# The SSD stage of a fused two-layer kernel: pacing of the group chains against the next group's GEMM

## The chip, the cores and the metric

One core of a Trainium2 chip runs the whole program. The metric is the device time of one launch in microseconds. Three runs of the kernel before gave 1353.03, 1350.03 and 1352.99 us, median 1352.99 us.

## The reference, cut to what matters

Two blocks run one after the other on 512 tokens of width 1024. The second block has an attention branch, a state-space (SSD) branch and a mixture of experts. The change touches only the SSD branch, which is (with the parts that do not matter here left out):

```python
xbc = silu(causal_depthwise_conv(xbc, conv_w, conv_b))       # 4 taps
xs, bs, cs = split(xbc, [2048, 2560])
dt = softplus(dt_raw + dt_bias); A = -exp(a_log)
y = ssd_chunked(xs.reshape(B, T, 32, 64), dt, A, bs, cs)     # 4 groups of 8 heads, state 128
y = y + d_skip * xs
yf = y * silu(z)                                             # per group of 512 columns:
y = yf * rsqrt(mean(yf * yf) + eps) * ssd_norm
merged = sigmoid(gate_a) * (y_attn @ w_attn_branch) + sigmoid(gate_b) * (y @ w_ssd_branch)
```

All values are float32. Every large matrix product is made of three products of rounded halves (high times high, high times low, low times high), so each weight tile is first split into a high and a low part.

## The kernel before, in words

The SSD branch is worked off in four groups g = 0 to 3 of 512 columns. For each group there are three kinds of work.

`ssd_gemm(g)` (line 1191) is the input projection: five units of `gemm_t` (line 210), each two output columns of 128 wide. Unit 0 gives B and C, units 1 and 2 give x, units 3 and 4 give z. A unit is 48 matmuls of 128x512 on TensorE (lines 224 to 226) and yields after every 12 of them with the planned time 12 x 0.217 = 2.604 us. Such a stretch of 12 matmuls is called a piece here, so a unit is 4 pieces and `ssd_gemm` 20. When a unit is complete its `done` function runs: for units 0 to 2 `conv_silu` (line 1169), which on VectorE is L1177, three L1183 and L1189 per output column, and for units 3 and 4 `silu_from` (L450 and L455 on VectorE per column).

`ssd_chain(g)` (line 1222) is the recurrence. Four time chunks c of 128 tokens pass through three stages in a software pipeline of six steps (`pipeline`, line 458). Stage s0 fetches the decay rows (DMA from `scr_a`, tile `ab`, two buffers) and transposes x and B on TensorE (L1245, L1249, L1247). Stage s1 subtracts per head on VectorE (eight L1265), takes the exponential on ScalarE (L1267) and multiplies (L1270). Stage s2 has the products L1278, L1283 and L1295 on TensorE, which VectorE evicts (L1280, L1290, L1297), and GpSimd adds (L1298). Then comes the gated norm: GpSimd multiplies y by z four times (L1303), ScalarE squares (L392), VectorE adds the squares (L393), TensorE sums them over partitions (L369, `rms_col`), VectorE and GpSimd make the reciprocal root (L372, L374), TensorE broadcasts it (L382), and VectorE scales and splits the four tiles (four L1311, four L356, beside ScalarE's L355) into `yh` and `yl`.

`ssd_branch(g)` (line 1320) is the output projection of a group from `yh` and `yl`: four GEMMs of 24 matmuls, 8 pieces in all.

The order in which this is written out comes from `mix(main, filler)` (line 32): the chain yields a need in planned microseconds, and pieces of the filler are written until the need is paid; a surplus is carried over. In `block2b` (line 1339) the filler of chain g is `ssd_branch(g - 1)` followed by `ssd_gemm(g + 1)`; `block2m` (line 1349) does the last chain, with `ssd_branch(2)`, two attention projections of 8 pieces each (`attn`) and the loads for them as filler. Each engine works through its own queue in order. The program is built with a planner (`schedule_with_timeline_sim`) that replays the written order and, on each engine, takes the earliest written instruction that it holds to be ready; so the order of a queue follows the written order, except that an instruction that the planner holds to be late is passed by later ones. The order is fixed when the program is built.

Of the kernel before, what the change touches and what calls it, by code (L numbers as in the profile page):

```python
# [24 lines left out]
KK = ([0, 1, 2, 3], [4, 5, 6, 7])  # L25

def run(gen):
    for _ in gen:
        pass


def mix(main, filler):

    debt = 0
    for need in main:
        debt += need
        while debt > 0:
            t = next(filler, None)
            if t is None:
                break  # L40
            debt -= t


class Ker:
# [1146 lines left out]
    def ssd_gemm(self, g, hh, hl, rb, rbh):  # L1191

        nc = self.nc
        u2 = lambda i: [("w2", 2 * (8 + 5 * g + i)), ("w2", 2 * (8 + 5 * g + i) + 1)]
        d = self.grp[g] = {}

        def bc_done(ps):
            d["b"], d["c"] = self.t2(), self.t2()
            self.conv_silu(ps, (16 + g, 20 + g), (d["b"], d["c"]), rb)

        def xs_done(i):
            def f(ps):
                if i == 0:
                    d["xs"], d["y"] = self.t8(), self.t8()
                self.conv_silu(ps, (4 * g + 2 * i, 4 * g + 2 * i + 1), (d["xs"][:, 2 * i], d["xs"][:, 2 * i + 1]), rb)
                for j in (2 * i, 2 * i + 1):
                    nc.scalar.activation(d["y"][:, j], d["xs"][:, j], AF.Copy, scale=self.pv("d_skip", 4 * g + j))
            return f

        d["z"] = self.mm[g % 2 * 4:g % 2 * 4 + 4]  # L1210

        def z_done(i):
            def f(ps):
                self.silu_from(ps, rbh, d["z"][2 * i:2 * i + 2])
            return f
        yield from self.gemm_t(u2(0), hh, hl, KK, bc_done)
        for i in range(2):
            yield from self.gemm_t(u2(1 + i), hh, hl, KK, xs_done(i))
        for i in range(2):
            yield from self.gemm_t(u2(3 + i), hh, hl, KK, z_done(i))  # L1220

    def ssd_chain(self, g, need):
        nc = self.nc
        d = self.grp[g]
        xs, y, bT, cT = d["xs"], d["y"], d["b"], d["c"]
# [76 lines left out]
        for k in range(4):  # L1302
            nc.gpsimd.tensor_tensor(y[k], d["y"][:, k], y[k], op=ALU.mult)  # L1303
            self.acc_sq(ssq, y[k], k == 0)
        yield need
        r = self.rms_col(ssq, NT, 512)
        yield 2.6
        pr = self.bcast_rows(r, NT)
        d["yh"], d["yl"] = [], []
        for k in range(4):  # L1310
# [27 lines left out]

    def block2b(self, hh, hl, rb, rbh):
        self.grp = {}  # L1340
        f = self.ssd_gemm(0, hh, hl, rb, rbh)
        mix(self.ssd_prep(), f)
        run(f)
        for g in range(3):
            f = chain(*([self.ssd_branch(g - 1)] if g else []), self.ssd_gemm(g + 1, hh, hl, rb, rbh))
            mix(self.ssd_chain(g, 4.0), f)
            run(f)

    def block2m(self):

        nc = self.nc
        yah, yal = [], []
        ma = self.mm

        def load():
            yt = [self.t8(F32R) for _ in range(2)]
            for k in range(8):
                t_ = self.t2()
                nc.sync.dma_start(t_, self.yad[k])
                h, l = self.split(t_, hi=yt[k // 4][:, k % 4])  # L1360
                yah.append(h)
                yal.append(l)
                yield 0

        def attn(g):
            for t_, i in zip(ma[2 * g:2 * g + 2], range(2)):
                nc.sync.dma_start(t_, self.gd[2 * g + i])

            def f(ps):
                for t_, p in zip(ma[2 * g:2 * g + 2], ps):  # L1370
                    nc.vector.scalar_tensor_tensor(t_, t_, 1.0, p, op0=ALU.add, op1=ALU.mult)
            yield from self.gemm_t([("wab", 2 * g), ("wab", 2 * g + 1)], yah, yal, KK, f)

        f = chain(self.ssd_branch(2), load(), attn(0), attn(1))
        mix(self.ssd_chain(3, 4.0), f)
        run(f)
        run(attn(2))
        run(attn(3))
        gb = []

        def fetch():
            t_ = self.t2()
            nc.sync.dma_start(t_, self.gd[8 + len(gb)])
            gb.append(t_)
        for _ in range(4):
            fetch()
        mh, ml, mt = [], [], []

        def merge(k):
            t_ = gb[k]  # L1390
            m = self.mB[k]
            nc.vector.scalar_tensor_tensor(m, t_, 1.0, m, op0=ALU.add, op1=ALU.mult)
            nc.vector.tensor_tensor(m, m, ma[k], op=ALU.add)
            if k % 4 == 0:
                mt.append(self.t8(F32R))
            h, l = self.split(m, hi=mt[k // 4][:, k % 4])
            mh.append(h)
            ml.append(l)
            if k < 4:
                fetch()  # L1400
        run(self.ssd_branch(3, lambda c: (merge(2 * c), merge(2 * c + 1))))
        return mh, ml
# [799 lines left out]
```

## Time and profile before

The span is cut into engines; a row of windows gives, for a stretch of the span, its length, the busy time of each engine with the number of instructions, the granted clock of TensorE as a share of full speed, the DMA share and the rate.

| | |
|---|---|
| median of 3 runs | 1352.99 us |
| the profiled execution | 1348.09 us |
| its span | 1346.1 us |
| TensorE busy | 1263.8 us, 94% |
| VectorE busy | 869.1 us, 65% |
| ScalarE busy | 506.3 us, 38% |
| GpSimd busy | 436.5 us, 32% |
| DMA, mean | 167 GB/s |

The SSD stage lies between about 555 us (first GEMM of group 0) and about 1020 us of the span; the chains of groups 0 to 3 begin at 611.3, 692.0, 792.7 and 893.1 us. After it come the output projection, the router and the experts, which read their weights at over 400 GB/s up to the end.

### The profile page before, as it was taken

What the parts mean: (1) busy time and instruction counts of PE and PEld (TensorE: products, weight loads), DVE (VectorE), ACT (ScalarE), POOL (GpSimd) and SP (SyncE); (2) the same over time, 40 slices, a digit from 0 to 9 for tenths busy, and PEclk for the clock granted to TensorE, in tenths of its full rate; (3) what the DMA queues carried; (4) which work ended last, traced back from release to release, by engine and by line L of the source; (5) the groups of instructions that cost most, each with busy time, mean ns of one, the idle gap of its engine ahead of it and who ended that gap; (6) DMA issues with size and microseconds to landing.
All of it is one profiled execution on the core that took longest, in us unless ns stands there. A gap on an engine that the chain in (4) does not pass through costs nothing.

```text
span 1346.1 us, 18784 instructions
## 1 busy us (share of the span) xinstructions
PE 1263.8 (94%) x6992; PEld 976.4 (73%) x6992; DVE 869.1 (65%) x1648; ACT 506.3 (38%) x938; POOL 436.5 (32%) x467
## 2 busy tenths in 40 slices
PE   5959999999999999999989899999999999999897
PEld 5858888999987888888767787787889744334223
DVE  5596765767998667687977887877683522111116
ACT  4545453345544455354442442443333211111011
POOL 5473134159343431122444234234415200000011
PEclk8979999999999999999989899899999899999999
DMA  7324232142233221134325235376420699999994
GB/s 249 110 65 141 63 120 97 51 156 80 65 117 110 79 95 63 56 112 133 90 83 133 78 102 126 110 246 174 140 106 37 234 403 417 401 415 415 415 414 182
DMA packets 87342, 224.86 MB, mean 167 GB/s; under 512 B 7840, under 2 KB 31040, under 8 KB 87248
## 3 DMA queue, kind: packets, MB, share of 16 engines
q1 hardware_dynamic: 79808, 203.08, 44.0%
q10 hardware_dynamic: 4992, 11.83, 2.3%
q0 software_dynamic: 2448, 8.72, 1.8%
q8 instruction: 56, 0.92, 0.3%
q14 instruction: 38, 0.31, 0.1%
HBM read 205.97 MB, written 17.63 MB: 166 GB/s over the span
## 4 chain that ended last, share of the span: by engine, by line
PE 63%; DVE 20%; DMA 10%; issue 4%; ACT 2%; POOL 1%; SPq 0%; ACTq 0%; DVEq 0%; POOLq 0%
PE pmm L224 9%; PE pmm L226 9%; PE pmm L225 9%; PE pmm L1740 7%; PE pmm L1761 5%; DMA t<-scr_a 4%; DVE t L1265 2%; PE paux L1078 2%; DVE t L1010 2%; DMA wr<-in_we_dram 2%; DMA tb<-in_we_dram 2%; DVE m L1009 1%; PE paux L1727 1%; DVE wlo L175 1%; PE pmm L242 1%
## 5 line engine op out<-in xcount | busy, mean ns | idle before, releaser
L175 POOL TENSOR_TENSOR wlo<-tb,whi 128x1024 fp32r<-128x1024 f32 x78 | 199.0, 2552 | 329.0 <-ACT whi L173 300.7
L224 PE MATMUL pmm<-tb,whi 128*128 128x512 f32 x600 | 240.0, 400 | 1.8 <-DVE t L903 1.8
L226 PE MATMUL pmm<-tb,wlo 128*128 128x512 f32 x600 | 239.1, 399 | 0.0
L225 PE MATMUL pmm<-tb,whi 128*128 128x512 f32 x600 | 238.8, 398 | 0.0
L173 ACT CAST whi<-tb 128x1024 fp32r<-128x1024 f32 x139 | 145.0, 1047 | 148.9 <-PE pmm L225 69.6
L224 PEld LDWEIGHTS pmm<-tb,whi 128*128 128x128 f32 x600 | 115.0, 192 | 25.4 <-DVE t L903 2.2
L226 PEld LDWEIGHTS pmm<-tb,wlo 128*128 128x128 f32 x600 | 115.1, 192 | 24.3 <-issue 0.5
L225 PEld LDWEIGHTS pmm<-tb,whi 128*128 128x128 f32 x600 | 114.9, 192 | 23.3 <-issue 0.4
L175 DVE TENSOR_TENSOR wlo<-tb,whi 128x1024 fp32r<-128x1024 f32 x61 | 81.8, 1343 | 26.0 <-ACT whi L173 25.8
L224 PE MATMUL pmm<-t,whi 128*128 128x512 f32 (+1 forms) x208 | 79.2, 393 | 12.4 <-DVE t L610 12.4
L225 PE MATMUL pmm<-t,whi 128*128 128x512 f32 (+1 forms) x208 | 80.3, 390 | 0.9 <-DVE t L356 0.8
L226 PE MATMUL pmm<-t,wlo 128*128 128x512 f32 (+1 forms) x208 | 80.2, 389 | 0.0
L1747 DVE SCALAR_TENSOR_TENSOR th<-th,pmm 128x256 f32<-128x256 f32 x16 | 6.7, 420 | 106.6 <-ACT th L1746 106.6
L1265 DVE TENSOR_SCALAR t<-t,acs 128x128 f32<-128x128 f32 x128 | 54.7, 493 | 19.6 <-DMA t<-scr_a 19.6
L1183 DVE SCALAR_TENSOR_TENSOR t<-cv,cwh,t 128x512 f32<-128x512 f32 x72 | 61.3, 901 | 0.3 <-ACT t L1180 0.3
L1740 PE MATMUL pmm<-wr,xe 128*64 128x512 f32 x200 | 57.8, 598 | 1.5 <-DMA wr<-in_we_dram 1.5
L1679 POOL COPY wcol<-wrow 32x2 f32<-32x2 f32 x64 | 11.9, 186 | 137.3 <-DVE y L1773 58.7
L334 PE MATMUL pmm<-whi,tb 128*128 128x256 f32 x192 | 54.7, 285 | 0.0
L336 PE MATMUL pmm<-whi,tb 128*128 128x256 f32 x192 | 54.5, 284 | 0.0
L224 PEld LDWEIGHTS pmm<-t,whi 128*128 128x128 f32 x208 | 39.8, 192 | 20.2 <-issue 13.0
L335 PE MATMUL pmm<-wlo,tb 128*128 128x256 f32 x192 | 54.3, 283 | 0.0
L1746 ACT ACTIVATE th<-pmm,wcol 128x256 f32<-128x256 f32 x16 | 7.6, 473 | 114.8 <-PE pmm L1740 56.1
(446 smaller groups left out, 2961.6 us busy)
## 6 DMA issues: line engine op xcount, KB each, us to landing
wr<-in_we_dram SPq DMA_DIRECT2D x82, 512.0 KB, 10.0
tb<-in_w_dram SPq DMA_DIRECT2D x78, 512.0 KB, 3.6
rx<-in_we_dram SPq DMA_DIRECT2D x55, 512.0 KB, 9.5
tb<-in_we_dram SPq DMA_DIRECT2D x55, 512.0 KB, 10.0
tb<-in_wo_dram SPq DMA_DIRECT2D x16, 512.0 KB, 3.9
tb<-in_wg_dram SPq DMA_DIRECT2D x16, 512.0 KB, 3.6
t<-scr_a SPq DMA_DIRECT2D x16, 512.0 KB, 6.4
tb<-in_wsb_dram SPq DMA_DIRECT2D x16, 512.0 KB, 3.6
```

Of the source, the lines that this page charges most:

```text
L173: nc.vector.tensor_copy(hi, raw) if dve_hi else nc.scalar.copy(hi, raw)
L175: f = lambda: (nc.gpsimd if pool_lo else nc.vector).tensor_tensor(lo, raw, hi, op=ALU.subtract)
L224: nc.tensor.matmul(ps[c][:, :n], hi[:, s], xh[k], start=first, stop=False)
L225: nc.tensor.matmul(ps[c][:, :n], hi[:, s], xl[k], start=False, stop=False)
L226: nc.tensor.matmul(ps[c][:, :n], lo[:, s], xh[k], start=False, stop=last)
L334: nc.tensor.matmul(o, xh[k][:, ts], hi[:, s], start=(k == 0 and t % 2 == 0), stop=False, **kw)
L335: nc.tensor.matmul(o, xh[k][:, ts], lo[:, s], start=False, stop=False, **kw)
L336: nc.tensor.matmul(o, xl[k][:, ts], hi[:, s], start=False, stop=(k == 7), **kw)
L1183: nc.vector.scalar_tensor_tensor(y, x[:, i:T + i], w(ct, i), y, op0=ALU.mult, op1=ALU.add)
L1265: nc.vector.tensor_scalar(h8(ab)[:, h], h8(ab)[:, h], self.acs[:, c, 8 * g + h:8 * g + h + 1], 0.0, op0=ALU.subtract, op1=ALU.min)
L1740: nc.tensor.matmul(pg[h * 64:h * 64 + 64], xe[d][:, e + h], w[:, j * 512:(j + 1) * 512], start=(d == 0), stop=(d == 7))
L1761: nc.tensor.matmul(py[q][h * 64:h * 64 + 64], ac[:, k, h * 64:h * 64 + 64], w[:, q * 512:(q + 1) * 512], start=(k == 0), stop=(k == 1))
```

## The change

`ssd_gemm` now returns a list of five generators, one for each unit. The chains of groups 0 to 2 have other needs: the six pipeline steps 4.8 us for group 0 and 7.0 us for groups 1 and 2 in place of 4.0; the wait between the sum of squares and `rms_col` 13.0 us in place of 4.0; the one between `rms_col` and `bcast_rows` 5.2 us in place of 2.6. The last 2.6 us stay. `ssd_branch(g - 1)` is written behind unit 0 of `ssd_gemm(g + 1)` and no longer ahead of it. The last group's chain keeps its 4.0, 4.0 and 2.6.

```diff
-        yield from self.gemm_t(u2(0), hh, hl, KK, bc_done)
-        for i in range(2):
-            yield from self.gemm_t(u2(1 + i), hh, hl, KK, xs_done(i))
-        for i in range(2):
-            yield from self.gemm_t(u2(3 + i), hh, hl, KK, z_done(i))
-
-    def ssd_chain(self, g, need):
+        return ([self.gemm_t(u2(0), hh, hl, KK, bc_done)] + [self.gemm_t(u2(1 + i), hh, hl, KK, xs_done(i)) for i in range(2)]
+                + [self.gemm_t(u2(3 + i), hh, hl, KK, z_done(i)) for i in range(2)])
+
+    def ssd_chain(self, g, need, late, mid=5.2):
...
             self.acc_sq(ssq, y[k], k == 0)
-        yield need
+        yield late
         r = self.rms_col(ssq, NT, 512)
-        yield 2.6
+        yield mid
         pr = self.bcast_rows(r, NT)
...
-        f = self.ssd_gemm(0, hh, hl, rb, rbh)
+        f = chain(*self.ssd_gemm(0, hh, hl, rb, rbh))
         mix(self.ssd_prep(), f)
         run(f)
         for g in range(3):
-            f = chain(*([self.ssd_branch(g - 1)] if g else []), self.ssd_gemm(g + 1, hh, hl, rb, rbh))
-            mix(self.ssd_chain(g, 4.0), f)
+            first, *rest = self.ssd_gemm(g + 1, hh, hl, rb, rbh)
+            f = chain(first, *([self.ssd_branch(g - 1)] if g else []), *rest)
+            mix(self.ssd_chain(g, 7.0 if g else 4.8, 13.0), f)
             run(f)
...
-        mix(self.ssd_chain(3, 4.0), f)
+        mix(self.ssd_chain(3, 4.0, 4.0, 2.6), f)
```

## Rows read from the trace of the kernel before

**Rows 1.** Window of chain 1: length; PE, PEld, DVE, ACT, POOL busy; clock; DMA.
```profile
692.00:792.70 100.70, 94.32 (x469) 76.14 (x468) 78.23 (x116) 42.32 (x63) 38.31 (x26) 0.97 0.36 98
```
**Rows 2.** Waits of PE, 611 to 985 us: total us, times, longest.
```profile
PE paux L369 <- DVE t L393: 12.3, 3, 6.0
PE pacc L1278 <- DVE t L1280: 4.1, 3, 1.9
...
PE paux L1247 <- DVE t L1297: 0.7, 1, 0.7
PE paux L1247 <- DVE t L1290: 0.5, 1, 0.5
```
**Rows 3.** Windows around the stretches with a lower granted clock.
```profile
675.00:685.00 10.00, 6.53 (x19) 5.51 (x20) 8.26 (x13) 5.15 (x8) 1.57 (x4) 0.50 0.36 102
746.00:754.00 8.00, 6.31 (x20) 5.35 (x21) 7.79 (x13) 2.14 (x4) 1.24 (x1) 0.57 0.42 131
828.00:832.50 4.50, 4.19 (x27) 3.82 (x28) 4.50 (x14) 0.46 (x1) 1.27 (x1) 0.62 0.22 64
849.00:856.50 7.50, 7.50 (x24) 6.16 (x24) 6.73 (x11) 3.62 (x5) 2.02 (x4) 0.54 0.31 92
```
**Rows 4.** Timeline of PE: start, us, instruction; in brackets idle before, releaser.
```profile
678.47 1.87 PE L369 MATMUL paux<-ones,t 128*128 128x1 f32 x8 [5.95 <-DVE t L393]
...
726.92 1.09 PE L1278 MATMUL pacc<-t,t 128*64 128x128 f32 x16 [1.24 <-DVE t L1280]
...
747.69 1.87 PE L369 MATMUL paux<-ones,t 128*128 128x1 f32 x8 [4.50 <-DVE t L393]
...
828.31 1.72 PE L1278 MATMUL pacc<-t,t 128*64 128x128 f32 x16 [1.88 <-DVE t L1280]
...
848.75 1.58 PE L369 MATMUL paux<-ones,t 128*128 128x1 f32 x8 [1.89 <-DVE t L393]
...
949.78 0.39 PE L226 MATMUL pmm<-t,wlo 128*128 128x512 f32 x1
...
950.46 0.39 PE L226 MATMUL pmm<-t,wlo 128*128 128x512 f32 x1
...
950.92 0.95 PE L369 MATMUL paux<-ones,t 128*128 128x1 f32 x8
```
**Rows 5.** Windows, L226 alone, four to a piece: PE, PEld busy (count).
```profile
611.30:654.40 43.10, 18.12 (x46) 8.45 (x45) 1.00 0.46 129
692.00:726.90 34.90, 12.80 (x32) 6.02 (x32) 1.00 0.47 121
...
611.30:672.40 61.10, 27.08 (x69) 12.78 (x68) 1.00 0.40 111
692.00:743.40 51.40, 20.59 (x52) 9.77 (x52) 1.00 0.43 108
```
**Rows 6.** Timeline of DVE around the ends of chains 0 and 1.
```profile
631.37 1.46 DVE L1265 TENSOR_SCALAR t<-t,acs 128x128 f32<-128x128 f32 x7 [2.50 <-DMA t<-scr_a]
...
663.50 5.92 DVE L1265 TENSOR_SCALAR t<-t,acs 128x128 f32<-128x128 f32 x8
...
743.63 4.00 DVE L393 TENSOR_TENSOR t<-t,t 128x512 f32<-128x512 f32 x3 [3.25 <-ACT t L392]
747.55 1.28 DVE L1177 TENSOR_TENSOR cv<-pmm,tb 128x512 f32<-128x512 f32 x2
...
749.88 2.73 DVE L1183 SCALAR_TENSOR_TENSOR t<-cv,cwh,t 128x512 f32<-128x512 f32 x4
...
759.21 2.72 DVE L1311 SCALAR_TENSOR_TENSOR mm<-mm,pvt,paux 128x512 f32<-128x512 f32 x4 [1.25 <-PE paux L382]
...
764.78 1.89 DVE L356 TENSOR_TENSOR t<-mm,t 128x512 fp32r<-128x512 f32 x3
```
**Rows 7.** Timeline of POOL: the four gate products of chain 0.
```profile
663.85 5.09 POOL L1303 TENSOR_TENSOR mm<-t,mm 128x512 f32<-128x512 f32 x4
```
**Rows 8.** Window after the stage, ahead of the experts' weight stream (DMA last).
```profile
1030.00:1040.00 10.00, 10.00 (x89) 10.00 (x88) 2.29 (x6) 2.87 (x8) 5.39 (x6) 1.00 0.01 2
```

## The prediction, made before the changed kernel was run

> **What bounds the kernel now.** I read the page first: TensorE is busy for 94% of the span, so inside the SSD stage its idle time and its slow time are what can be won. Second the window of one chain, 692.0 to 792.7 us: of 100.7 us VectorE is busy 78.2 and TensorE 94.3 [rows 1]; no engine but these two is near its limit. Third the waits of TensorE over the four chains [rows 2]: everything is behind VectorE, 12.3 us of it at the three `rms_col` products (L369), 4.1 us at L1278, and 0.7 and 0.5 us at L1247. Fourth the same waits in order [rows 4]: 5.95, 4.50 and 1.89 us at the L369 of chains 0, 1 and 2, 1.24 and 1.88 us at L1278 of chains 1 and 2. The remaining 1.0 us at L1278 and no wait at L369 belong to chain 3, which keeps its needs.
>
> Fifth the clock. In the stretches behind the larger waits the granted clock is half of full speed (the 1.2 GHz level) for part of the row [rows 3]. A row of d us at mean clock c holds (1-c) x d us of lost work: 5.0, 3.4, 1.7 and 3.45 us. Where TensorE stood idle at that level nothing was lost: in the first row it was idle from 675.0 to 678.5, which takes half of 3.5 us off (3.3 left), in the second I take 0.4 off (3.0 left). L369 shows the same: 1.87 us behind a wait, 0.95 us at full speed [rows 4].
>
> Lost to waits and clock: chain 0: 0.7 + 5.95 + 3.3 = 10.0; chain 1: 0.5 + 1.24 + 4.50 + 3.0 = 9.2; chain 2: 1.88 + 1.7 + 1.89 + 3.45 = 8.9. Together 28.1 us. The rest of TensorE's work in the stage is the same matmuls after the change.
>
> **Where things are written now and then.** A piece is planned at 2.604 us; three of its matmuls take 950.46 - 949.78 = 0.68 us [rows 4], so 12 take 2.7 us. With a need of 4.0 the six steps are paid after 2, 4, 5, 7, 8 and 10 pieces and L369 is written after 11. With 4.8 (chain 0): 2, 4, 6, 8, 10, 12, then L369 after 17 and the broadcast L382 after 19 of 20. With 7.0 (chains 1 and 2): 3, 6, 9, 11, 14, 17, then L369 after 22 and L382 after 24 of 28. The last L1278 belongs to step six, so it is written after 8 pieces before, 10 and 14 then.
>
> Where they really stood in the queue is seen by counting L226 [rows 5]. Chain 0: the last L1278 after 46/4 = 11.5 pieces, L369 after 69/4 = 17.25, both later than written; chain 1: 8 and 13. So the planner had already moved L369 back by 6 and 2 pieces, and still put it too early: the true VectorE was later than planned.
>
> **Chains 1 and 2, steps.** A step gets 2.8 pieces (7.7 us) and not 1.67 (4.5 us). The waits at L1278 and L1247 come from evictions queued behind other VectorE work by at most 1.88 us; 3.2 us more per step cover them. Gain 0.5 + 1.24 + 1.88 + 1.7 (clock) = 5.3 us, bounds 0 and 5.3. I take all of it.
>
> **Chains 1 and 2, norm.** From the last L1278 to the L369 that got its data were 747.69 - 726.92 = 20.8 and 848.75 - 828.31 = 20.4 us [rows 4]. Then there are 8 pieces between them, 21.8 us, and about 2 us of L1278 and its neighbours: 23.8, so 3 us in hand. Against it: in this stretch the unit that is complete after 16 pieces now puts its convolution on VectorE ahead of L393: two L1177 (1.28 us), six L1183 (2.73/4 each, 4.1 us), two L1189, of the size of L1177 (1.3): 6.6 us [rows 6]. VectorE had idle time there, of which the row of L393 shows 3.25 us. So the data come after 20.6 + 6.6 less 0 to 5 us, 22 to 27, and TensorE waits 0 to 3.4 us per chain; the waits of 1.88 us and more were each followed by a half-clock stretch [rows 3, 4]. I take 1.5 us and 1 us of clock. Chain 1: 9.2 - 2.5 = 6.7 won; chain 2: 8.9 - 2.5 = 6.4 won.
>
> **Chain 0.** Its queue distance hardly changes: L369 stood at 17.25 pieces and is now written at 17; the data needed 678.47 - 654.4 = 24 us from the last L1278 [rows 4, 5]. If that stays at 11.5 pieces, 5.5 pieces and 2 us cover 17 us as before, and the wait of 6 us stays. If it comes at its written 10 pieces, 7 pieces (19.1) and 2 cover 21 us, 3 are left. I take the middle, 4.4 us and 2.7 us of clock: 3 won, bounds 0 and 10.
>
> The late part of that distance has a cause that the pace does not remove. Seven L1265 took 1.46 us, but eight took 5.92 us where GpSimd's four L1303 ran from 663.85 for 5.09 us [rows 6, 7]. These L1265 belong to the next chain; they are set off by the same release of `ab` buffers, and ScalarE's squares stood behind their exponential. The Trainium skill has a rule for it (SBUF — State Buffer, Who interferes with whom): a VectorE operation that uses both port pairs, a tensor-scalar among them, and a GpSimd operation shut each other out for whole instructions, whichever was issued first. By it these 4.2 us would be paid wherever the two meet, also under the norm's own tail, and the sum would be nearer to the second rival's; the durations agree with it.
>
> **The order of `ssd_branch`.** Behind unit 0 it gets 4 pieces (10.9 us) more for `yh` and `yl`, for groups 0 and 1. The tail runs from L1311 at 759.21 to the end of the last L356 at 766.67, 7.5 us, and 1 us of L382 [rows 6]. Chain 0: from its L382 one piece of the old filler, then 4 new ones, 13.6 us: hidden. Chain 1 has 4 + 4 pieces: hidden. B and C of the next group are held longer; the 14 buffers of their kind just hold them, the convolution's two and the chain's eight. I put this at 0, bounds 0 and 3.
>
> For group 2 there is no such unit: `block2m` is unchanged and starts with s0 and `ssd_branch(2)`, 4 pieces (10.9 us) and 1 us after L382. The tail needs 8.5 us, and in the last 8 pieces (21.8 us) VectorE has the convolution (6.6), L393 (4.0), two z units (2.6 each, sized as L1177), the tail (5.2) and two splits of 1.3: 23.6 us. Before, such a tail had some 33 us of GEMM behind it (759.2 to 792.7 in chain 1) [rows 1, 6]. I take 2 us of wait and 0.5 of clock, bounds 0 and 12 (VectorE late by the whole of its overrun and ten slow L1265).
>
> **Behind the stage.** DMA stands idle at 1030 to 1040 us [rows 8]; the experts' weights begin after the stage, so what is won arrives at the end.
>
> **Sum.** -3 - 6.7 - 6.4 + 2.5 = -13.6 us. The profiled execution would go from 1348.1 to 1334.5. It is 4.9 us under the median of the runs, 1352.99, which I carry: 1339.4.
>
> **Rivals.**
> First, all waits go: 28.1 us less, 1325. For it: all of them are behind VectorE, which at 78.2 of 91.5 us without the waits [rows 1, 4] is still below its limit. Against: 85% leaves little for bursts, and chain 0.
>
> Second, the lateness travels: L369 waits for data in any case, since the planner counts VectorE too fast, whatever is written. Then only the step waits go (5.3) and group 2's tail costs 2.5: 1350. For it: the 2 to 6 pieces by which L369 had been moved back in vain.
>
> Third, slower: the norm of group 2 comes late into `block2m`. Place: the first matmul of `ssd_branch(2)`. Price: up to 12 us of wait and 3.4 of clock, as after the largest wait [rows 3], while chains 0 to 2 win 5.3 at their steps alone: 1353 + 10 = 1363. It decides once the tail ends more than 12 us after L382 and the waits at L369 stay. For it: 23.6 us of VectorE work in 21.8. Against: z units are light, and the planner can pass the late branch with s0.
>
> **How the numbers follow.** The forecast (1330 to 1347) 0.53; all waits go 0.17; the lateness travels (1347 to 1356) 0.16; slower 0.14. A measurement tells 0.3%, 4 us, from no change. Faster (below 1349): 0.53 + 0.17 + 0.07 = 0.77; within: 0.09 and 0.02 of the last = 0.11; slower 0.12. The range 1325 to 1354 leaves out the ends of the first and third rival.
>
> **What would show it.** Right: no or short waits at L369 of chains 1 and 2, no idle TensorE at L1278 there, granted clock 1.00 throughout these chains, some wait left at L369 of chain 0. Wrong: waits at L369 as long as now in spite of the later place, a wait of `ssd_branch(2)` for L356 above 4 us, or new waits behind VectorE in the pieces that carry both chain and convolution.

## The result, and the profile after

The changed kernel takes 1330.53 us (median of four runs, 1327.60 to 1333.59) against 1352.47 us: a ratio of 0.9845, 95% interval 0.9822 to 0.9868. The profiled execution took 1331.22 us, its span 1329.6 us. The forecast was 1339.4 us in a range of 1325 to 1354: right in direction and range. Against the profile of before it said 13.6 us less; the two profiled executions differ by 16.9 us. A later series of six runs gave 0.9883 (0.9849 to 0.9917), so one series tells little about single microseconds. For the parts I therefore use the trace: from the first transpose of chain 0 to the L369 of chain 3 TensorE has the same products in every kernel here. This stretch, called the stage below, went from 339.7 us (611.26 to 950.92) to 322.5 us (611.74 to 934.27).

Waits of TensorE from 611 to 985 us of the changed kernel (engine, tile and line, waited for: total us, times, longest), the counterpart of [rows 2]. Chain lines have moved: L1278 is now L1275, L1247 L1244, L1265 L1262, L1303 L1300, L1280 L1277, L1295 L1292, L1297 L1294, L1290 L1287.

```profile
PE paux L369 <- DVE t L393: 2.6, 2, 1.5
PE paux L1244 <- DVE t L1287: 2.3, 1, 2.3
PE paux L382 <- POOL rr L374: 1.8, 2, 0.9
PE pacc L1275 <- DVE t L1277: 1.0, 1, 1.0
```

12.3 us at L369 have become 2.6, and L1275 waits only in chain 3, as before. New is the wait for GpSimd's root at L382, and the one wait at L1244, in chain 0, is 2.30 us where L1247 waited 0.75 us before. The timeline of TensorE in the changed kernel, the counterpart of [rows 4], gives the places:

```profile
644.52 0.49 PE L1244 MATMUL paux<-t,t 128*128 128x128 f32 x2 [2.30 <-DVE t L1287]
...
684.36 1.02 PE L369 MATMUL paux<-ones,t 128*128 128x1 f32 x8 [1.49 <-DVE t L393]
...
763.68 1.05 PE L369 MATMUL paux<-ones,t 128*128 128x1 f32 x8 [1.16 <-DVE t L393]
...
773.68 1.16 PE L382 MATMUL paux<-cst,rr 128*128 128x128 f32 x8 [0.86 <-POOL rr L374]
...
866.83 1.16 PE L382 MATMUL paux<-cst,rr 128*128 128x128 f32 x8 [0.93 <-POOL rr L374]
```

The windows of the changed kernel (length, then PE, PEld, DVE, ACT, POOL busy, clock, DMA): chain 1 as in [rows 1], chain 2, and the places of the waits as in [rows 3].

```profile
693.50:783.10 89.60, 87.58 (x456) 70.68 (x455) 74.50 (x114) 42.11 (x62) 34.37 (x26) 1.00 0.35 101
783.10:876.20 93.10, 92.03 (x474) 74.46 (x473) 77.78 (x119) 38.58 (x53) 36.21 (x25) 1.00 0.45 133
640.00:650.00 10.00, 7.70 (x43) 5.67 (x42) 10.00 (x20) 4.16 (x5) 3.69 (x3) 0.83 0.40 107
680.00:690.00 10.00, 8.51 (x35) 6.74 (x34) 8.80 (x11) 5.34 (x8) 7.26 (x4) 0.83 0.29 73
760.00:770.00 10.00, 8.84 (x44) 7.13 (x43) 9.79 (x16) 6.16 (x10) 0.86 (x4) 1.00 0.37 105
```

Chains 1 and 2 run at full clock throughout; chain 0 still has two rows at 0.83, which is (1 - 0.83) x 10 = 1.7 us each. So chain 0 loses 2.30 + 1.49 + 3.4 = 7.2 us (10.0 before), chain 1 2.0 (9.2), chain 2 1.1 with a remainder of 0.14 at its L369 (8.9). That is 17.8 of the stage's 17.1 us, the clock being read to a tenth or two.

### The profile page after: what moved, and what is told of

Its sections match the earlier page's. It is cut to its first block, busy times and chain, and to the rows that moved or that the text cites. A ratio compares the mean times of both kernels' runs of the same rounds, so it can differ in the third digit from the quotient of the medians.

```text
span 1329.6 us, 18774 instructions
## 1 busy us (share of the span) xinstructions
PE 1258.4 (95%) x6992; PEld 970.4 (73%) x6992; DVE 861.8 (65%) x1648; ACT 506.9 (38%) x938; POOL 440.0 (33%) x467
## 5 line engine op out<-in xcount | busy, mean ns | idle before, releaser
L175 POOL TENSOR_TENSOR wlo<-tb,whi 128x1024 fp32r<-128x1024 f32 x78 | 199.6, 2560 | 319.5 <-ACT whi L173 293.1
L226 PE MATMUL pmm<-tb,wlo 128*128 128x512 f32 x600 | 236.8, 395 | 0.0
L226 PEld LDWEIGHTS pmm<-tb,wlo 128*128 128x128 f32 x600 | 113.8, 190 | 23.8 <-issue 0.2
L175 DVE TENSOR_TENSOR wlo<-tb,whi 128x1024 fp32r<-128x1024 f32 x61 | 82.2, 1349 | 27.8 <-ACT whi L173 27.4
L226 PE MATMUL pmm<-t,wlo 128*128 128x512 f32 (+1 forms) x208 | 80.0, 388 | 0.0
L1262 DVE TENSOR_SCALAR t<-t,acs 128x128 f32<-128x128 f32 x128 | 41.8, 393 | 26.9 <-DMA t<-scr_a 26.7
L1183 DVE SCALAR_TENSOR_TENSOR t<-cv,cwh,t 128x512 f32<-128x512 f32 x72 | 58.5, 868 | 0.3 <-ACT t L1180 0.3
L224 PEld LDWEIGHTS pmm<-t,whi 128*128 128x128 f32 x208 | 40.1, 193 | 20.0 <-issue 12.8
```

What stands on the lines that cost most here:

```text
L175: f = lambda: (nc.gpsimd if pool_lo else nc.vector).tensor_tensor(lo, raw, hi, op=ALU.subtract)
L224: nc.tensor.matmul(ps[c][:, :n], hi[:, s], xh[k], start=first, stop=False)
L226: nc.tensor.matmul(ps[c][:, :n], lo[:, s], xh[k], start=False, stop=last)
L1183: nc.vector.scalar_tensor_tensor(y, x[:, i:T + i], w(ct, i), y, op0=ALU.mult, op1=ALU.add)
L1262: nc.vector.tensor_scalar(h8(ab)[:, h], h8(ab)[:, h], self.acs[:, c, 8 * g + h:8 * g + h + 1], 0.0, op0=ALU.subtract, op1=ALU.min)
```

## The experiments

Stage times of all kernels, and of each the part that belongs to chain 3, whose needs and filler no edit changes. The ratios are to the kernel before, run in the same series:

| kernel | order of `ssd_branch` | steps | norm needs | gate product | stage us | of it chain 3 | ratio (95%) |
|---|---|---|---|---|---|---|---|
| before | old | 4.0 | 4.0, 2.6 | GpSimd | 339.7 | 57.8 | 1 |
| changed | new | 4.8 / 7.0 | 13.0, 5.2 | GpSimd | 322.5 | 58.0 | 0.9845 (0.9822 to 0.9868) |
| changed, repeated | new | 4.8 / 7.0 | 13.0, 5.2 | GpSimd | 325.1 | 60.3 | 0.9883 (0.9849 to 0.9917) |
| e1 | new | 4.0 | 4.0, 2.6 | GpSimd | 328.8 | 57.9 | 0.9931 (0.9907 to 0.9956) |
| e2 | new | 4.0 | 13.0, 5.2 | GpSimd | 327.7 | 57.0 | 0.9906 (0.9876 to 0.9935) |
| e3 | new | 4.8 / 7.0 | 4.0, 2.6 | GpSimd | 322.4 | 57.4 | 0.9889 (0.9853 to 0.9925) |
| e4 | old | 4.8 / 7.0 | 13.0, 5.2 | GpSimd | 334.2 | 57.3 | 0.9985 (0.9965 to 1.0006) |
| e5 | old | 4.8 / 7.0 | 13.0, 5.2 | GpSimd, taps left out | 340.9 | 62.7 | 0.9949 (0.9926 to 0.9971) |
| e6 | old | 4.0 | 4.0, 2.6 | VectorE | 328.8 | 59.6 | 0.9894 (0.9857 to 0.9930) |
| e7 | new | 4.8 / 7.0 | 13.0, 5.2 | VectorE | 321.9 | 58.1 | 0.9852 (0.9811 to 0.9893) |
| e8 | new | 5.6 / 8.0 | 8.0 or 9.0, 7.8 | GpSimd | 332.4 | 62.9 | 0.9894 (0.9858 to 0.9930) |
| e9 | new | 4.0 | 4.0, 2.6 | VectorE | 326.0 | 58.2 | 0.9870 (0.9842 to 0.9898) |
| e10 | new | 4.0 / 7.0 | 13.0, 5.2 | VectorE | 318.7 | 57.8 | 0.9840 (0.9812 to 0.9869) |

A stage is read from one profiled execution, and that is not always a middling one: those of e1 (1334.02 us, median 1341.00), e4 (1342.16, 1347.25) and e10 (1325.89, 1330.03) are the fastest of their series, that of e5 (1348.04, 1344.02) is the slowest. The two profiles of the changed kernel differ by 2.6 us, so a difference of that size says nothing.

The theory at the outset was that of the prediction: the norm that comes later wins most, the slower steps the rest, and the order nothing. The edits of the first four, on the changed kernel:

```diff
# e1
-            mix(self.ssd_chain(g, 7.0 if g else 4.8, 13.0), f)
+            mix(self.ssd_chain(g, 4.0, 4.0, 2.6), f)
# e2
+            mix(self.ssd_chain(g, 4.0, 13.0), f)
# e3
+            mix(self.ssd_chain(g, 7.0 if g else 4.8, 4.0, 2.6), f)
# e4
-            f = chain(first, *([self.ssd_branch(g - 1)] if g else []), *rest)
+            f = chain(*([self.ssd_branch(g - 1)] if g else []), first, *rest)
```

**e1, the order alone.** Expected:

> New order of ssd_branch alone, needs 4.0, 4.0, 2.6 as before. In the built queue L369 of chains 0, 1, 2 stands after 17.17, 34.67 and 63.75 pieces (before: 17.17, 33.17, 61.58; after the whole change: 19.58, 42.00, 70.00). Theory 1 (the later norm is what won) and theory 2 (the slower steps are what won): both expect the waits at L369 to stay, 2 to 6 us each, and a time within 4 us of before (1348 to 1356). Rival, theory 3 (the place of ssd_branch won): the time falls by 10 us or more, and the waits at L369 of chains 1 and 2 go.

Measured: stage 10.9 us shorter. TensorE's timeline in e1:

```profile
676.16 1.87 PE L369 MATMUL paux<-ones,t 128*128 128x1 f32 x8 [5.95 <-DVE t L393]
...
722.77 1.10 PE L1280 MATMUL paux<-t,bt 128*128 128x512 f32 x2 [1.19 <-DVE t L1248]
...
747.97 1.05 PE L369 MATMUL paux<-ones,t 128*128 128x1 f32 x8 [2.56 <-DVE t L393]
```

Chain 0, which has no branch in its filler, waits 5.95 us to the digit as before. Chain 1's 4.50 have become 2.56, chain 2 has no wait at all. Counted from first transpose to first transpose, chain 2 takes 92.1 us (100.4 before) and chain 1 99.8 (101.4): in chain 1 new waits stand beside the shorter one, 0.81 us at L1242, 0.76 at L1244 and 1.19 at L1280. The rival that I took least seriously, the order, is what wins here.

**e2, the later norm alone.** Expected:

> New order, steps 4.0 for all groups as before, norm needs 13.0 and 5.2 as in the change. Theory 1 (the need of 13 us holds L369 back until its data are there): the waits at L369 of chains 1 and 2 and their half-clock stretches go, some 12 us less than before, about 1340; the step waits at L1278 stay. Theory 2 (L369 stands where the planner holds its data to be ready, and the written need only matters if it is later): the built queue has L369 at 17.17, 35.00, 63.75 pieces, as with the order alone, so the time is that of the order alone within 2 us and the waits at L369 stay.

Measured: 1.1 us less in the stage than e1, 0.9906 against 0.9931 with overlapping intervals. L369 of chain 0 waits 5.97 us, that of chain 1 0.74 us, later by a third of a piece in the queue; what was won there is 1.8 us of wait, not the 12 us of theory 1.

**e3, the slower steps without the later norm.** Expected:

> New order, steps 4.8 and 7.0 as in the change, norm needs 4.0 and 2.6 as before. Theory 1: the L369 waits of chains 1 and 2 come back with 4 us each and clock, only the step waits (5 us) are won: about 1347. Theory 2: the built queue has L369 at 19.58, 41.67, 69.67 pieces (19.58, 42.00, 70.00 with the whole change) and L382 one piece earlier, so the time is that of the whole change plus 0 to 3 us, 1330 to 1334, L369 waits under 2.5 us each, and the waits at L382 for the GpSimd root grow by 1 to 2.7 us each.

Measured: the stage of the changed kernel (322.4 and 322.5). TensorE's timeline in e3:

```profile
685.92 1.02 PE L369 MATMUL paux<-ones,t 128*128 128x1 f32 x8 [1.42 <-DVE t L393]
...
764.97 1.05 PE L369 MATMUL paux<-ones,t 128*128 128x1 f32 x8 [1.79 <-DVE t L393]
...
859.45 0.72 PE L369 MATMUL paux<-ones,t 128*128 128x1 f32 x5 [1.04 <-DVE t L393]
```

The written 13 us hardly matter: the planner puts L369 where it holds the sum of squares to be ready, after 41.67 and 69.67 pieces, and the need moves it by a third of a piece. Theory 2 holds for L369; the longer waits at L382 that it also named did not come.

**e4, all needs, the old order.** Expected:

> All needs of the change, ssd_branch ahead of the first GEMM unit as before. Theory A: the new place hides the norm's tail; without it the first products of ssd_branch(0) stand right behind L382 (20.00 pieces) and wait for L356 by 8.5 us of tail less 1 to 2 us of s0, and those of ssd_branch(1) by 0 to 2 us: 6 to 12 us with the clock more than the whole change, 1337 to 1343. Theory B: the planner passes the late branch with other work, or VectorE is early enough: within 3 us of the whole change, 1328 to 1334.

Measured: 11.7 us more in the stage than the changed kernel, the ratio is back at 0.9985. But not by theory A's way: there is no wait of the branch's products for L356. Chain 0's L382 waits 1.50 us for GpSimd's root, and the waits of chains 1 and 2 are at L369 again, though it stands after 42.00 and 70.00 pieces as in the changed kernel:

```profile
770.82 1.87 PE L369 MATMUL paux<-ones,t 128*128 128x1 f32 x8 [4.01 <-DVE t L393]
...
869.17 1.87 PE L369 MATMUL paux<-ones,t 128*128 128x1 f32 x8 [3.93 <-DVE t L393]
```

VectorE shows why. First its timeline in e4 around the end of chain 1 (last L1275 on TensorE at 742.82):

```profile
742.90 4.05 DVE L1183 SCALAR_TENSOR_TENSOR t<-cv,cwh,t 128x512 f32<-128x512 f32 x6
746.88 0.67 DVE L1277 TENSOR_TENSOR t<-pacc,t 128x512 f32<-128x512 f32 x1
...
749.69 0.68 DVE L1294 TENSOR_TENSOR t<-paux,t 128x512 f32<-128x512 f32 x1
...
750.89 6.87 DVE L1262 TENSOR_SCALAR t<-t,acs 128x128 f32<-128x128 f32 x8
...
761.11 4.06 DVE L1183 SCALAR_TENSOR_TENSOR t<-cv,cwh,t 128x512 f32<-128x512 f32 x6
```

and in the changed kernel (last L1275 at 738.55):

```profile
739.71 0.68 DVE L1277 TENSOR_TENSOR t<-pacc,t 128x512 f32<-128x512 f32 x1
740.77 0.69 DVE L1294 TENSOR_TENSOR t<-paux,t 128x512 f32<-128x512 f32 x1 [0.39 <-PE paux L1292]
746.83 3.79 DVE L1262 TENSOR_SCALAR t<-t,acs 128x128 f32<-128x128 f32 x8 [5.36 <-DMA t<-scr_a]
...
753.96 4.06 DVE L1183 SCALAR_TENSOR_TENSOR t<-cv,cwh,t 128x512 f32<-128x512 f32 x6
...
761.36 2.27 DVE L393 TENSOR_TENSOR t<-t,t 128x512 f32<-128x512 f32 x3
```

With the branch ahead, unit 0 is complete after 12 pieces and its six L1183 stand in front of the last evictions, which end 5.4 us after the last L1292; with unit 0 ahead, its convolution was over at 719.26 and they end 0.7 us after it. Between these points and L369 VectorE is busy 24.75 of 26.0 us in e4:

```profile
745.00:771.00 26.00, 21.98 (x98) 17.87 (x97) 24.75 (x30) 11.24 (x16) 13.84 (x11) 0.97 0.30 93
```

and 16.31 of 23.0 us in the changed kernel (same columns):

```profile
740.70:763.70 23.00, 21.84 (x98) 17.73 (x96) 16.31 (x24) 10.00 (x15) 11.48 (x9) 1.00 0.41 115
```

That is theory D: the order takes one of the three convolutions off VectorE where the chain ends, and puts it near the chain's beginning (703.05 to 719.26 in chain 1 of the changed kernel), where TensorE waits for nothing.

**e5, theory D by itself:** e4 without three taps of the convolution of B and C of groups 1 to 3.

```diff
-            for i in range(3):
+            for i in range(0 if ct >= 17 and ct not in (20,) else 3):
```

> The branch-first kernel (e4: 1347.25 us, span 1340.5, waits at L369 1.04, 4.01, 3.93 us), with the three taps L1183 left out in the convolution of B and C of groups 1 to 3 (part of the computation is left out). The queue of TensorE for chains 1 and 2 is the same as in e4 (L369 after 42.00 and 70.00 pieces). Theory D (ssd_branch ahead puts a third unit's convolution onto VectorE just before the norm; its load is the price): 6 L1183, 4 to 5 us, less per chain, so the L369 waits of chains 1 and 2 fall to under 1.5 us, their half-clock stretches go, and the time falls by 8 us or more against e4, to about 1338. Rival F (the place of ssd_branch costs in another way, by its evictions or its late operands): the waits stay at 3 to 4 us, the time falls by under 3 us.

```profile
681.78 1.84 PE L369 MATMUL paux<-ones,t 128*128 128x1 f32 x8 [6.90 <-DVE t L393]
...
773.18 1.43 PE L369 MATMUL paux<-ones,t 128*128 128x1 f32 x8 [1.95 <-DVE t L393]
...
869.60 1.05 PE L369 MATMUL paux<-ones,t 128*128 128x1 f32 x8 [1.38 <-DVE t L393]
```

In chains 1 and 2, whose queue on TensorE is e4's, the waits halve (4.01 to 1.95, 3.93 to 1.38), and the last evictions end 2.1 and 1.5 us after the last L1292 in place of 5.4 and 5.3. So D is borne out there, if not to the size expected. The whole time fell by about 5 us against e4 (0.9949 and 0.9985 of the kernel before, with intervals that overlap a little), not by 8 or more. Two things stand against the gain: the planner, with less VectorE work to reckon with, moved L369 of chain 0 ahead (18.17 pieces, 19.58 in e4), and it waits 6.90 us in place of 1.04; and chain 3 has a wait of 2.92 us of the kind shown under e8. So the stage of this one profile is longer than e4's, by 5.0 us in chain 0 and 5.4 in chain 3, though chain 2 is 4.3 us shorter.

**e6, the kernel before with the gate products on VectorE.**

```diff
-            nc.gpsimd.tensor_tensor(y[k], d["y"][:, k], y[k], op=ALU.mult)
+            nc.vector.tensor_tensor(y[k], d["y"][:, k], y[k], op=ALU.mult)
```

> The kernel before, with the four gate products L1303 on VectorE and not on GpSimd. Theory C (L1303 on GpSimd shuts VectorE's eight L1265 out, 6 us in place of 1.7, and ScalarE's squares behind them): the L1265 beside it take under 2.5 us, the squares start earlier, VectorE has 2.7 us more of its own; the waits at L369 (5.95, 4.50, 1.89) fall by 2 us or more each and the time by 6 to 12 us. Rival (VectorE's load alone decides): 2.7 us more per chain, the waits grow by 1 to 3 us each, the time by 3 to 10 us.

Measured: ratio 0.9894, the stage 10.9 us shorter, with 2.5 us more of own work on VectorE per chain. TensorE's timeline in e6:

```profile
675.95 1.05 PE L369 MATMUL paux<-ones,t 128*128 128x1 f32 x8 [1.66 <-DVE t L393]
...
742.32 1.05 PE L369 MATMUL paux<-ones,t 128*128 128x1 f32 x8 [1.16 <-DVE t L393]
...
820.03 1.09 PE L1278 MATMUL pacc<-t,t 128*64 128x128 f32 x16 [2.18 <-DVE t L1280]
```

5.95, 4.50 and 1.89 us at L369 [rows 4] are 1.66, 1.16 and none. In chain 0 most of this is not earlier data: they come 22.9 us after the last L1278 (24.0 before), but the planner put L369 after 18.33 pieces and not 17.17, which is 3.2 us. In chains 1 and 2 L369 stands a third of a piece nearer to the last L1278 than before, and the data come 16.5 and 17.6 us after it (20.7 and 20.4 before). VectorE at the end of chain 1 in e6, to set against [rows 6]:

```profile
733.18 2.50 DVE L1303 TENSOR_TENSOR mm<-t,mm 128x512 f32<-128x512 f32 x4 [1.39 <-POOL t L1298]
736.76 3.32 DVE L1265 TENSOR_SCALAR t<-t,acs 128x128 f32<-128x128 f32 x8 [1.08 <-DMA t<-scr_a]
739.99 2.28 DVE L393 TENSOR_TENSOR t<-t,t 128x512 f32<-128x512 f32 x3
```

Theory C holds in chains 1 and 2: the products on GpSimd (5.09 us) had drawn eight L1265 out to six us, and the squares behind them. From the start of the products to the end of L393 chain 1 takes 9.1 us, 12.8 us before (734.82 to 747.63). The edit changes three things at once, and this run does not weigh them: the products themselves take 2.50 us, the L1265 come behind them, and ScalarE's squares (until 737.20) now stand ahead of the exponential (740.16). The L1265 take 3.32 us and not under 2.5 as expected; here they lie beside a weight split on GpSimd (L175, from 736.22 for 2.40 us). With GpSimd idle eight take 1.66 us, as in chain 1 of the kernel before:

```profile
729.39 1.66 DVE L1265 TENSOR_SCALAR t<-t,acs 128x128 f32<-128x128 f32 x8 [1.42 <-DMA t<-scr_a]
```

**e7, the same in the changed kernel.**

> The changed kernel with the gate products on VectorE. L369 stands after 20.25, 42.00, 70.00 pieces (19.58, 42.00, 70.00 without). Theory C: here the L1262 beside the products cost 3.8 and 3.5 us in place of 1.7, so 2 us each come back and 2.7 us are added: within 2 us of the changed kernel, waits at L369 0 to 2 us. Rival (VectorE's load alone): waits at L369 of chains 1 and 2 grow to 3 to 4 us with half clock, 8 us or more slower than the changed kernel.

Measured: stage 321.9 us, ratio 0.9852: no difference from the changed kernel, as theory C said. That nothing more is to be won there fits the rows of the changed kernel under e4: the convolution of unit 1 (L1183 from 753.96) lies between the products and L393 in any case.

**e8, still slower steps.**

```diff
+            mix(self.ssd_chain(g, 8.0 if g else 5.6, 9.0 if g else 8.0, 7.8), f)
```

> The changed kernel with still slower steps: 5.6 us for group 0, 8.0 us for groups 1 and 2, norm needs 8.0 or 9.0 and 7.8. The last L1292 of chains 1 and 2 stands after 36 and 64 pieces (34 and 62), L369 after 42.33 and 70.33 (42 and 70), L382 a tenth of a piece later. Theory of the prediction (more TensorE work per step hides VectorE): waits at L369 and L382 of chains 1 and 2 (2.0 and 0.9 us) and of chain 0 go or shrink, 2 to 6 us less than the changed kernel. Theory D (what counts is the VectorE work between the last L1275 and L369, 24 to 25 us of it in the changed kernel): only 6.3 pieces, 17 us and 2 us, are left for it, so waits of 2 to 5 us come back at L369 and the time is 4 to 14 us above the changed kernel.

```profile
663.56 2.08 PE L1292 MATMUL paux<-t,t 128*128 128x128 f32 x8 [3.07 <-DVE t L1287]
...
764.37 1.05 PE L369 MATMUL paux<-ones,t 128*128 128x1 f32 x8 [2.21 <-DVE t L393]
...
860.05 1.05 PE L369 MATMUL paux<-ones,t 128*128 128x1 f32 x8 [2.21 <-DVE t L393]
```

The waits of 2.21 us at L369 are those that theory D expected. The stage is 9.9 us longer, but 4.9 us of that are chain 3. There two L356, which prepare an operand of the attention projection, stand beside the gate products and a weight split on GpSimd (the L356 before them, at 925.93, took 0.69 us), and TensorE waits for them; in order GpSimd, VectorE, TensorE:

```profile
926.75 5.05 POOL L1300 TENSOR_TENSOR mm<-t,mm 128x512 f32<-128x512 f32 x4
...
927.34 7.91 DVE L356 TENSOR_TENSOR t<-t,t 128x512 fp32r<-128x512 f32 x2 [0.72 <-ACT t L355]
...
934.71 0.51 PE L225 MATMUL pmm<-t,whi 128*128 128x512 f32 x1 [2.90 <-DVE t L356]
```

The other 5.0 us lie in chains 0 to 2. By the whole time e8 is not clearly slower than the changed kernel (0.9894 against 0.9845 and 0.9883). Chain 1 now ends at 36 pieces, right where unit 1's convolution is on VectorE. Of the three paces tried with the new order, 4.0 (e1), 7.0 (changed) and 8.0, chains 0 to 2 are shortest at 7.0 (271.0, 264.5 and 269.5 us up to the first transpose of chain 3), where the chain ends between two convolutions; e1 and e8 also differ in the norm needs and in group 0.

**The changed kernel again, e9 and e10**, in one series. e9 is e7's kernel with needs 4.0, 4.0, 2.6; e10 is e7's with 4.0 in place of 4.8 for group 0.

> The changed kernel once more, beside the two that follow on the same chip: a ratio of 0.982 to 0.987 to the kernel before by every theory.

> Of the change only the new place of ssd_branch; needs 4.0, 4.0, 2.6 as before; the four gate products on VectorE. If theories C and D (the products on GpSimd hold VectorE up; the place of ssd_branch frees it when the chain ends) explain the gain, these two alone give at least what the whole change gives: waits at L369 of 1 to 2.5 us for chain 0, 0 to 2 us for chains 1 and 2, ratio to before 0.980 to 0.987. If the slower steps and the later norm are needed as well: 0.988 or more, with waits of 2 us and more at L1275, L1242 or L369 of chains 1 and 2.

> The changed kernel with the gate products on VectorE, and the steps of group 0 at 4.0 us in place of 4.8 (norm needs 13.0 and 5.2). With the products on GpSimd, 4.0 and 4.8 cost group 0 much the same (7 to 10 us). By theory C the wait of 6 us at L369 of group 0 was the products' doing, so at 4.0 it falls to 1 to 2.5 us and the 2.3 to 2.8 us at L1244 go too: 2 to 6 us less than the changed kernel, ratio to before 0.978 to 0.984. If group 0's steps matter by themselves: L369 or L1275 of chain 0 waits 4 us or more, 0.985 or more.

e9: order and gate product alone win 13.6 us of the stage, against the changed kernel's 17.1 and 14.5; by the whole time the two are level, 1334.28 and 1335.35 us in this series. So it is not shown that the slower steps are needed as well. What they would have to remove is in e9's chain 1, waits at L1242, L1275 and L1244 and a granted clock of 0.66 from 720 to 730, none of which the changed kernel has there; TensorE in e9:

```profile
678.66 1.38 PE L369 MATMUL paux<-ones,t 128*128 128x1 f32 x8 [1.68 <-DVE t L393]
...
720.78 1.98 PE L1275 MATMUL pacc<-t,t 128*64 128x128 f32 x16 [1.95 <-DVE t L1267]
```

e10 has the shortest stage, 318.7 us, and 1330.03 us beside 1335.35 us for the changed kernel in the same series; the intervals of the ratios still touch (0.9812 to 0.9869, 0.9849 to 0.9917). As in e6 the planner put L369 of chain 0 later than before, after 18.33 pieces. Its waits of TensorE:

```profile
PE paux L369 <- DVE t L393: 3.4, 3, 1.7
PE pacc L1275 <- DVE t L1277: 1.0, 1, 1.0
PE paux L1244 <- DVE t L1294: 1.0, 1, 1.0
```

## Why the prediction was right, and where it was not

**The inventory held.** 28.1 us of waits and half clock were there to be won, and every one that went is found in them: VectorE's lateness was the bound, and what was won arrived at the end.

**The terms came out near, chain 0's by luck.** Chain 1: 6.7 forecast, 7.2 found. Chain 2: 6.4 and 7.8. The data of these two were to come 22 to 27 us after the last L1278; they come 25.1 and 24.1 us after it, and TensorE has eight pieces in between, as forecast (34.00 to 42.00 and 62.00 to 70.00). Chain 0: 3 and 2.8, but not in the way forecast. L369 was to go on waiting 4.4 us at 17 pieces; the planner put it after 19.58 and it waits 1.49, and what that won beyond the forecast went to the wait of 2.30 us at L1244 and the half clock behind it. The term for the norm of group 2 in `block2m`, 2.5 us, was mis-sized: chain 3 takes 58.0 us to its L369 (876.25 to 934.27) and took 57.8, so 0.2.

**The step that failed is "The order of `ssd_branch` ... I put this at 0".** By itself it wins 10.9 us of the stage (e1), and without it the needs win 5.5 of 17.1 (e4). That the sum came out all the same is in part luck: most of what it put down to the needs comes, at this pace, only with the order. The working counted the unit that is complete after 16 pieces against the norm, which is right for the new order (units complete after 4, 16 and 20), and never asked about the old one, in which unit 0 is complete after 12 and its convolution stands ahead of the slower chain's last evictions (e4). The order was priced by what `yh` and `yl` need, where it gains nothing; at the new pace its price lies with VectorE.

**The later norm was credited with what it does not do.** In chains 1 and 2 L369 stands where it is written, after 22 pieces of the chain, but not because of the need of 13 us: with the pace of 7.0 the planner moves it to within a third of a piece of the same place without that need (e3). The prediction itself showed that the planner had moved L369 back by 6 and 2 pieces, and used that only for chain 0 and a rival. The second rival was right that the written place decides little, and wrong that the waits then stay: with the slower steps and the new order the planner's place is eight pieces behind the last L1275 (5.2 and 5.4 before), and that hides the data but for 1.16 and 0.14 us.

**The port rule was underrated.** Eight L1265 at 5.92 us beside L1303 were seen and given to a rival. e6 shows what hung on them in the kernel before: taking the products off GpSimd wins as much of the stage as the order does, 10.9 us each, part of it in chain 0 by a later place of L369. The two do not add up (e9: 13.6). The rule of the Trainium skill (SBUF — State Buffer, Who interferes with whom) says that such a pair excludes each other for whole instructions; the trace agrees (6.41 and 6.19 us for eight beside the products in chains 1 and 2, 1.66 us with GpSimd idle). In chains 1 and 2 the changed kernel does not remove the meeting (3.79 and 3.54 us), it gives it time.

**Left open.** How the order wins at the old pace of 4.0 (e1) is not shown. Theory D is not the reason there: in the kernel before the convolution of unit 0 (L1177) begins only as L393 ends, at 747.55 in chain 1 [rows 6] and at 848.62 in chain 2. Most of e1's gain is in chain 2, whose data come 15.4 us after the last L1275 (20.4 before) and whose last evictions end 0.7 us after the last L1292. In the kernel before they end 2.9 us after it, behind two evictions of the branch (L1331) and a weight split (L175); this is read from VectorE's queue and not tested. The 2.6 us between the two profiles of the changed kernel lie mostly at chain 3 (58.0 and 60.3 us), whose same wait of 1.02 us was followed by half clock in one of them and not in the other.

## What to carry to other kernels

Where two streams of work share a busy engine, count that engine's work between the point where the data are born and the point where they are wanted, for the old order and the new one: an edit that seems to reorder one engine's queue can have its price on another. A planner that moves late instructions back can make written waits inert; look at the built queue before crediting one. And an operation given to a side engine to relieve the main one can hold the main one up: try it there before making room for it.

## What the runs showed of the hardware

The eight L1265 beside the gate products do not take a fixed toll, they end with them: products until 668.94, 739.91 and (changed kernel, L1300 from 744.52 for 5.03 us) 749.55, the L1265 until 669.42, 740.38 and 750.62, whether they began 0.35 and 0.85 us before or 2.3 us after the products. The toll is not the gate products' alone: in chain 1 of the kernel before, eight L1265 took 3.91 us from 719.91, beside a weight split on GpSimd (L175, from 720.57 for 2.38 us), against 1.66 us with GpSimd idle.

The clock fell after shorter waits than the kernel before had shown: the waits of 2.30 and 1.49 us in chain 0 of the changed kernel were both followed by a row at 0.83, those of 1.16 and 0.86 us by none. The wait of about 1.02 us at the last L1278 (now L1275) of chain 3 stands in all thirteen profiles; half clock followed it in two, the second of the changed kernel and e6 (a row at 0.83 each).
